# An mLSTM and sparse-attention layer step on one core: 66 of its 68 TensorE transposes are done by VectorE 32x32 turns and GpSimd copies, used three to five tiles later

## The chip, the cores and the metric

The kernel runs on one core of one Trainium2 chip. The metric is the device time of one execution in microseconds (us). PE is TensorE (PEld its weight loads), DVE is VectorE, ACT is ScalarE, POOL is GpSimd and SP is SyncE.

## The reference, cut to what matters

A step of a streaming encoder layer for 256 new frames (the prompt) and 32 frames of a running stream (the sample); every weight is shared by both.

```python
p = x @ w_in                                     # x: (288, 1024); about 12,000 columns
# branch B: 8 heads x 128, each query keeps its top keys by an indexer score
logits = where(kept, q @ k.T * 128**-0.5 + rel_bias, -inf)
o_b = softmax(logits) @ v
# branch A: mLSTM, 4 heads x 256, gates i and f
s = (q @ k.T) * wmat                             # decay weights, causal
h = (s @ v + (q * inter) @ C) / max(|s.sum + inter * q.n|, exp(-m))
C_new = decay * C + (w_s * k).T @ v              # n_new likewise
hn = (h - mean(h)) * rsqrt(var(h) + eps) * g     # per head and frame
branch_a = hn * sigmoid(o) * silu(z_a);  branch_b = o_b * silu(z_b)
y = layer_norm(alpha * x + (sigmoid(g_a) * (branch_a @ w_out_a)
                            + sigmoid(g_b) * (branch_b @ w_out_b)) @ w_o)
```

## The kernel before

The weights are cut into 117 tiles of 128 columns (or 128 rows), named by what they make and a number: `sm`, `qi`, then `qb`/`kb` by head, `vb`, `qa`/`ka`, `va`, `zb`, `oa`/`za`, `gb`/`wb`, `ga`/`wa`, `wo`. The main loop takes one tile at a time; a **slot** is one turn of it. Each f32 weight tile is split into a high part (`wh`, made by ACT in `split_hi`, L133) and a low part (`wl`, the rest, made by DVE in `split_lo`, L140), both of type fp32r, and each product is three matmuls: high by high, high by low of the other side, low by high (L901 to L903, 24 matmuls per tile). In slot t ACT makes `wh` of tile t+3 and DVE makes `wl` of tile t+2; there are two pairs of buffers (4 buffers of tag `wh`, 4 of `wl`). The slot before's product is then taken out of PSUM (`evac`), and the matmuls of tile t follow.

Halfway through a tile's 24 matmuls PE does side work: `side()` runs one step of every generator that is under way (`procs`), up to its next `yield`. A `yield` therefore means "in the next tile". Every engine takes its instructions in the order of this written program; what crosses engines is held by semaphores, and a buffer of a shared tag is taken again only when its last readers are done.

The side work that the change touches:

- `attn_sample`: softmax of the sample's logits (two groups of four heads, `lgs`), six PE transposes into PSUM (`aspt`, L517 and L519), ACT copies into `pst`, one tile later 48 small matmuls with the values (`os`, L531), two transposes back (`ost`, L540).
- `attn(h)`, eight heads, one started every two and a half tiles: logits (`al`), exponentials, normalised on DVE (L565), then one tile later three PE transposes (`apt`, L570); ACT takes the high part out of PSUM (`pth`, L573) and the plain part (`pt`, L574), DVE the low part (`ptl`, L575); one tile later the values' matmuls (`av`).
- `mlstm(h)`, four heads, one every four tiles: its normalised result `hn` (128 frames by 256) is transposed by four PE transposes (`ht`, L643) and multiplied on DVE out of PSUM (`ba`, L645).
- `k_weighted(h)`: four PE transposes (`kt`, L660) of the keys `kaT`, in the first four `wo` slots.
- `mlstm_sample`: two transposes of the sample's keys (`vks`, L742), the high and low parts of keys and values stacked in `stk` (the low parts by DVE, L756), the head norm with a power on POOL (L707), eight matmuls and eight DVE updates of the state (`stC`), two transposes at the end (`hts`, L785).

Of the kernel before, what the change touches and what calls it, by code (L numbers as in the profile page):

```python
# [10 lines left out]
F32 = mybir.dt.float32  # L11
# [9 lines left out]
TP = 256  # L21
# [65 lines left out]
def body(ctx, tc, a, o):  # L87
# [19 lines left out]
    def start(slot, gen):  # L107
        at(slot, procs.append, gen)

# [384 lines left out]
    def attn_sample():  # L494
# [5 lines left out]
        for g in two:  # L500
            lg = sb(f"lgs{g}", [128, 384], tag="lg", bufs=3)[:, :T]
            lgs.append(lg)
            st = sb(f"sts{g}", [128, 4], tag="st", bufs=3)
            dve.scalar_tensor_tensor(lg, q[g][:, :T], scale, bms[:, g], op0=OP.mult, op1=OP.add)
            dve.tensor_reduce(st[:, 0:1], lg, axis=AX.X, op=OP.max, negate=True)
            act.activation(lg, lg, AF.Exp, bias=st[:, 0:1], accum_out=st[:, 2:3])
            dve.reciprocal(st[:, 1:2], st[:, 2:3])
            dve.tensor_scalar(lg, lg, st[:, 1:2], None, op0=OP.mult)
        pts = [sb(f"pst{g}", [128, 384], tag="kw", bufs=2) for g in two]
        for g in two:  # L510
            dve.memset(pts[g][:, 256:384], 0.0)
        yield
# [7 lines left out]
        for g in two:  # L520
            act.copy(pts[g][:, 0:256], p[g][:, 0:256])
            for i in range(4):
                r = slice(32 * i, 32 * i + 32)
                act.copy(pts[g][r, 256 + 32 * i:288 + 32 * i], p[g][:TS, 256 + 32 * i:288 + 32 * i])
# [18 lines left out]
    def attn(h):  # L543
# [56 lines left out]
    def mlstm(h):  # L600
# [33 lines left out]
        yield  # L634
        while "state_done" not in store or cur[0] <= POS["za", 2 * h + 1] + 1:
            yield
        bah, bal = branch_a()
        ba = []
        for vb in range(2):
            p = bank(f"ht{h}{vb}")  # L640
            c = slice(128 * vb, 128 * vb + 128)
# [9 lines left out]

    def k_weighted(h):
# [4 lines left out]
        p = bank(f"kt{h}")  # L657
        for kd in range(2):
            for b in range(2):
                pe.transpose(p[:, 256 * b + 128 * kd:256 * b + 128 * kd + 128],  # L660
                             kaT[:, 2 * h + kd, 128 * b:128 * b + 128], ident)
        for b in range(2):
            k = slice(256 * b, 256 * b + 256)
            act.activation(kwh[:, b], p[:, k], AF.Identity, scale=gnat[:, b, 2, h:h + 1])
            dve.scalar_tensor_tensor(kwl[:, b], p[:, k], gnat[:, b, 2, h:h + 1], kwh[:, b].bitcast(F32),
                                     op0=OP.mult, op1=OP.subtract)
# [54 lines left out]
    def mlstm_sample():  # L721
# [3 lines left out]
        tail = sb("tail", [128, 2, 4, TS], tag="ba", bufs=2)  # L725
        for kd in range(2):
            pool.tensor_copy(tail[:, kd], kaT[:, kd:8:2, TP:T])
# [10 lines left out]
        p = bank("vks")  # L738
        v1 = sb("v1s", [128, 258], tag="v1s")
        dve.memset(v1[:, 256:258], 1.0)  # L740
        for kd in range(2):
            pe.transpose(p[:, 128 * kd:128 * kd + 128], tail[:, kd].rearrange("p h t -> p (h t)"), ident)  # L742
        act.copy(v1[:, 0:256], lazy["vas"])
        kw = sb("kws", [128, 258], tag="sw", bufs=2)
        dve.tensor_scalar(kw[:, 0:256], p[:, 0:256], gns[:, 2:3], None, op0=OP.mult)
# [4 lines left out]
        for i, (src, n) in enumerate(((kw, 256), (v1, 258))):  # L750
            act.copy(hi[i][:, :n], src[:, :n])
            for h in range(AH):
# [3 lines left out]
                dve.tensor_tensor(dst[lo:lo + 32], src[r, :n], hi[i][r, :n].bitcast(F32), OP.subtract)  # L756
# [26 lines left out]
        p = bank("hts")  # L783
        for vb in range(2):
            pe.transpose(p[:, 128 * vb:128 * vb + 128], hn[:, 0, 128 * vb:128 * vb + 128], ident)  # L785
        ba = sb("bas", [128, 2, 4, TS], tag="ba", bufs=2)
        for vb in range(2):
            dve.tensor_tensor(ba[:, vb], p[:, 128 * vb:128 * vb + 128].rearrange("p (h t) -> p h t", h=4),
                              GT[:, vb:8:2, TP:T], OP.mult)
# [278 lines left out]
    start(POS["zb", 2], mlstm_sample())  # L1068
    for h in range(AH):
# [129 lines left out]
```

## Time and profile before

| what | value |
|---|---|
| time, median of 3 runs | 425.77 us (425.51 to 426.06) |
| the profiled execution's own time | 425.51 us |
| its span in the trace | 423.8 us (1.7 us of the time lie outside) |
| PE busy | 417.5 us (99%) |
| DVE busy | 299.8 us (71%) |
| ACT busy | 227.1 us (54%) |
| POOL busy | 27.1 us (6%) |
| TensorE's granted clock over the span | 0.998 of full |

Busy time is the time in which an engine had an instruction under way; matmuls overlap each other, so the duration of one is longer than the step from one to the next. The step is read from the chain of work, the views that list times of start, and not from mean durations.

### The profile page before, as it was taken

Reading aid. Unit: us, or ns where it says so; the run is one execution under the profiler, and the core shown is the slowest. Engines: PE = TensorE matmul, PEld = TensorE weight load, DVE = VectorE, ACT = ScalarE, POOL = GpSimd, SP = SyncE. Lnnn points to the kernel's source line nnn. Section 1 sums busy time; section 2 is a strip of 40 time slices with the busy share of each in tenths; the row PEclk is TensorE's granted clock in tenths of the full one; section 3 lists DMA queues with packets and bytes.
Section 4 is the critical chain, followed back from the end, with each engine's and each line's share of the span. In section 5 each row is a group of like instructions: output and inputs, shape, how many; then the busy total and the mean of one; then the engine's idle time right before and its main releaser. Section 6 shows DMA issues by size and latency. Waiting matters only on the chain.

```text
span 423.8 us, 8154 instructions
## 1 busy us (share of the span) xinstructions
PE 417.5 (99%) x3180; PEld 394.3 (93%) x3180; DVE 299.8 (71%) x595; ACT 227.1 (54%) x443; POOL 27.1 (6%) x60
## 2 busy tenths in 40 slices
PE   8999999999999999999999999999999999999995
PEld 7999999778999998779999999999999999998864
DVE  5769999995856566675999987786444455665674
ACT  6775465326666565558796366545334344446402
POOL 0200011000400000000001101100000000000031
PEclk9999999999999999999999999999999999999999
DMA  8987979377954620437444454444645548433014
GB/s 310 378 296 215 316 252 330 123 199 265 388 164 149 215 87 0 174 126 298 150 149 150 151 181 167 151 149 150 198 150 171 177 150 281 154 125 124 28 38 150
DMA packets 31587, 78.70 MB, mean 186 GB/s; under 512 B 10412, under 2 KB 13724, under 8 KB 30748
## 3 DMA queue, kind: packets, MB, share of 16 engines
q1 hardware_dynamic: 30684, 76.86, 53.4%
q10 hardware_dynamic: 864, 1.32, 0.9%
q8 instruction: 25, 0.41, 0.4%
q14 instruction: 14, 0.11, 0.1%
HBM read 72.38 MB, written 7.68 MB: 189 GB/s over the span
## 4 chain that ended last, share of the span: by engine, by line
PE 97%; DVE 1%; POOLq 0%; ACT 0%; DVEq 0%; issue 0%
PE pj L902 22%; PE pj L901 22%; PE pj L903 22%; PE yn L949 5%; PE pj L968 3%; PE pj L919 2%; PE pj L918 2%; PE pj L917 2%; PE warm_p L151 1%; PE vap L917 1%; PE vbp L917 1%; PE vap L925 1%; PE vbp L925 1%; PE vbp L919 1%; PE vbp L918 1%; PE vap L919 1%
## 5 line engine op out<-in xcount | busy, mean ns | idle before, releaser
L133 ACT CAST wh<-wst 128x1024 fp32r<-128x1024 f32 x112 | 117.8, 1052 | 139.5 <-PE pj L902 68.2
L901 PE MATMUL pj<-xh,wh 128*128 128x288 f32 x576 | 171.1, 297 | 0.0
L902 PE MATMUL pj<-xl,wh 128*128 128x288 f32 x576 | 169.9, 295 | 0.0
L903 PE MATMUL pj<-xh,wl 128*128 128x288 f32 x576 | 169.7, 295 | 0.0
L140 DVE TENSOR_TENSOR wl<-wst,wh 128x1024 fp32r<-128x1024 f32 x112 | 136.2, 1218 | 30.6 <-ACT wh L133 30.2
L901 PEld LDWEIGHTS pj<-xh,wh 128*128 128x128 f32 x576 | 108.3, 188 | 0.5 <-issue 0.4
L902 PEld LDWEIGHTS pj<-xl,wh 128*128 128x128 f32 x576 | 108.3, 188 | 0.0
L903 PEld LDWEIGHTS pj<-xh,wl 128*128 128x128 f32 x576 | 108.2, 188 | 0.0
L902 PE MATMUL pj<-bbl,wh 128*128 128x288 f32 x64 | 18.9, 296 | 0.0
L903 PE MATMUL pj<-bah,wl 128*128 128x288 f32 x64 | 18.9, 296 | 0.0
L902 PE MATMUL pj<-bal,wh 128*128 128x288 f32 x64 | 18.9, 295 | 0.0
L901 PE MATMUL pj<-bbh,wh 128*128 128x288 f32 x64 | 18.9, 295 | 0.0
L901 PE MATMUL pj<-bah,wh 128*128 128x288 f32 x64 | 18.8, 294 | 0.0
L903 PE MATMUL pj<-bbh,wl 128*128 128x288 f32 x64 | 18.8, 294 | 0.0
L949 PE MATMUL yn<-wh,mxh 128*128 128x512 f32 x32 | 13.0, 406 | 0.0
L917 PE MATMUL pj<-wh,xh 128*128 128x512 f32 x32 | 12.9, 404 | 0.0
L949 PE MATMUL yn<-wl,mxh 128*128 128x512 f32 x32 | 12.6, 395 | 0.1
L919 PE MATMUL pj<-wh,xl 128*128 128x512 f32 x32 | 12.7, 395 | 0.0
L918 PE MATMUL pj<-wl,xh 128*128 128x512 f32 x32 | 12.6, 395 | 0.0
L949 PE MATMUL yn<-wh,mxl 128*128 128x512 f32 x32 | 12.6, 395 | 0.0
L901 PEld LDWEIGHTS pj<-bbh,wh 128*128 128x128 f32 x64 | 12.0, 188 | 0.0
L903 PEld LDWEIGHTS pj<-bah,wl 128*128 128x128 f32 x64 | 12.0, 188 | 0.0
(482 smaller groups left out, 674.5 us busy)
## 6 DMA issues: line engine op xcount, KB each, us to landing
wst<-in_w SPq DMA_DIRECT2D x112, 512.0 KB, 4.1
wst_k<-in_first SPq DMA_DIRECT2D x7, 464.0 KB, 4.3
rscr<-rrow SPq DMA_DIRECT2D x2, 768.0 KB
out_k<-kbT SPq DMA_DIRECT2D x1, 1152.0 KB
stC<-in_state_C SPq DMA_DIRECT2D x1, 1028.0 KB, 5.8
out_C_sample<-stC SPq DMA_DIRECT2D x1, 1028.0 KB
bm<-rscr SPq DMA_DIRECT2D x1, 1024.0 KB
ckT<-in_cache_k SPq DMA_DIRECT2D x1, 1024.0 KB
```

What stands on the lines that cost most here:

```text
L133: act.copy(split[t][0], stage[t])
L140: dve.tensor_tensor(wl, stage[t], wh.bitcast(F32), OP.subtract)
L151: pe.matmul(wp[:, :256], lhsT=warm[:, :128], rhs=warm, start=True, stop=True)
L901: pe.matmul(p[:, :T], lhsT=wh[:, c], rhs=h[:, k], start=(k == 0), stop=False)
L902: pe.matmul(p[:, :T], lhsT=wh[:, c], rhs=l[:, k], start=False, stop=False)
L903: pe.matmul(p[:, :T], lhsT=wl[:, c], rhs=h[:, k], start=False, stop=(k == KT - 1))
L917: pe.matmul(banks[i], lhsT=xh[:, k, r], rhs=wh[:, c], start=(k == 0), stop=False)
L918: pe.matmul(banks[i], lhsT=xh[:, k, r], rhs=wl[:, c], start=False, stop=False)
L919: pe.matmul(banks[i], lhsT=xl[:, k, r], rhs=wh[:, c], start=False, stop=(k == KT - 1))
L925: pe.matmul(banks[4][32 * i:32 * i + 32, 0:256].rearrange("p (g c) -> p g c", g=g), lhsT=xs0[:, kk], rhs=w[:, i], start=(kk == 0), stop=(k ...
L949: pe.matmul(p, lhsT=x[:, k, r], rhs=w[:, c], start=first and i == 0, stop=last and i == 2)
L968: pe.matmul(p[t][:, new], lhsT=w[:, 128 * t:128 * t + 128], rhs=x[:, k, new], start=(k == 0 and w is wh and x is xh), stop=(k == KT - 1 an ...
```

## The change

`carry` copies 32x32 blocks across groups of 32 partitions on POOL: four source groups by four target groups, 16 copies. A full transpose is now a DVE `transpose`, which turns each 32x32 block in its place, and then `carry`, which puts the blocks where they belong. All transposes of the list above but `ost` are done in this way, and each is used later by some `yield`s: the sample's probabilities 5 tiles after the softmax (3 before), a head's probabilities 3 tiles after the normalisation (1 before), `hn` 4 tiles after its turn. The sample's keys are turned at the start of `mlstm_sample` and used 4 tiles later (the whole of it now runs 3 tiles later from there on). The prompt's keys are turned in place by a new generator `k_natural`, 4 copies per tile over 16 tiles from `gb` 6, so that `k_weighted` has no PE work. The low parts in `stk` are made by POOL in place of DVE.

```diff
+    quads = tuple(slice(32 * i, 32 * i + 32) for i in range(4))
+    def carry(out, turned, rows):
+        for i in rows:
+            for k in range(4):
+                pool.tensor_copy(out(quads[k], quads[i]), turned(quads[i], quads[k]))
...
 attn_sample:
             dve.tensor_scalar(lg, lg, st[:, 1:2], None, op0=OP.mult)
+            dve.transpose(bms[:, g], lg)
...
-        yield
-        yield
-        p = [bank(f"aspt{g}") for g in two]
-        for g in two:
-            for b in two:
-                pe.transpose(p[g][:, 128 * b:128 * b + 128], lgs[g][:, 128 * b:128 * b + 128], ident)
-        for g in two:
-            pe.transpose(p[g][:TS, 256:384], lgs[g][:, 256:T], ident)
         for g in two:
-            act.copy(pts[g][:, 0:256], p[g][:, 0:256])
+            pt = pts[g][:, 0:256].rearrange("p (b k) -> p b k", b=2)
+            turned = bms[:, g, 0:256].rearrange("p (b k) -> p b k", b=2)
+            carry(lambda p, c: pt[p, :, c], lambda p, c: turned[p, :, c], range(4))
             for i in range(4):
-                r = slice(32 * i, 32 * i + 32)
-                act.copy(pts[g][r, 256 + 32 * i:288 + 32 * i], p[g][:TS, 256 + 32 * i:288 + 32 * i])
+                pool.tensor_copy(pts[g][quads[i], 256 + 32 * i:288 + 32 * i], bms[quads[i], g, 256:T])
+        yield
+        yield
+        yield
+        yield
         yield
         q = [bank(f"os{g}") for g in two]
...
 attn(h):
-        for i, s in enumerate(parts):
+        turned = bm[:, h].rearrange("p (c k) -> p c k", c=3)
+        for i, s, c in ((0, parts[0], slice(128, 384)), (1, parts[1], slice(0, 128))):
             dve.tensor_scalar(lg[:, s], lg[:, s], st[:, 2 + i:3 + i], None, op0=OP.mult)
+            dve.transpose(bm[:, h, c], lg[:, s])
+        ptf = sb(f"pt{h}", [128, 384], tag="kw", bufs=2)
+        pt3 = ptf.rearrange("p (c k) -> p c k", c=3)
+        carry(lambda p, c: pt3[p, :, c], lambda p, c: turned[p, :, c], range(4))
+        yield
+        yield
         yield
         vh, vl = two_parts(f"v{h}", vn[:, 0, 128 * h:128 * h + 128], "vph", "vpl")
-        p = bank(f"apt{h}")
-        for i, c in enumerate((256, 0, 128)):
-            pe.transpose(p[:, 128 * i:128 * i + 128], lg[:, c:c + 128], ident)
-        pt = sb(f"pt{h}", [128, 128], tag="sw", bufs=2)
+        pt = ptf[:, 256:384]
         ph, pl = (sb(f"pt{n}{h}", [128, 256], F32R, tag="hn", bufs=2) for n in "hl")
-        act.copy(ph, p[:, 0:256])
-        act.copy(pt, p[:, 256:384])
-        dve.tensor_tensor(pl, p[:, 0:256], ph.bitcast(F32), OP.subtract)
+        act.copy(ph, ptf[:, 0:256])
+        dve.tensor_tensor(pl, ptf[:, 0:256], ph.bitcast(F32), OP.subtract)
...
 mlstm(h):
+        for b in range(2):
+            dve.transpose(turned[:, b], hn[:, b])
...
+        carry(lambda p, c: hT[p, :, :, c], lambda p, c: turned[p, :, :, c], range(4))
+        for _ in range(4):
+            yield
...
-            for b in range(2):
-                pe.transpose(p[:, 128 * b:128 * b + 128], hn[:, b, c], ident)
-            dve.tensor_tensor(ba[vb], p[:, :TP], GT[:, 2 * h + vb, :TP], OP.mult)
+            dve.tensor_tensor(ba[vb], hn[:, vb], GT[:, 2 * h + vb, :TP], OP.mult)
...
+    def k_natural():
+        for h in range(AH):
+            k = kaT[:, 2 * h:2 * h + 2, 0:TP]
+            turned = sb(f"kn{h}", [128, 2, TP], tag="kw", bufs=2)
+            for i in range(2):
+                dve.transpose(turned[:, i], k[:, i])
...
+            for i in range(4):
+                carry(lambda p, c: kn[p, :, :, c], lambda p, c: turned[p, :, :, c], (i,))
+                yield
...
 mlstm_sample:
-                dve.tensor_tensor(dst[lo:lo + 32], src[r, :n], hi[i][r, :n].bitcast(F32), OP.subtract)
+                pool.tensor_tensor(dst[lo:lo + 32], src[r, :n], hi[i][r, :n].bitcast(F32), OP.subtract)
...
-        while cur[0] <= POS["za", 7] + 1:
+        while cur[0] <= POS["za", 7] + 6:
...
+    start(POS["gb", 6], k_natural())
```

**What stands in a row now, on PE.** This is PE in the tile that held the first head's transposes, before: `pj` is the tile's product, `apt` the transposed probabilities of head 0.

```order
L902 MATMUL pj_1774<-xl,wh_1606 128x288
L903 MATMUL pj_1774<-xh,wl_1607 128x288
L570 MATMUL apt_1791<-cst,lg_1659 128x128 x3
L901 MATMUL pj_1774<-xh,wh_1606 128x288
L902 MATMUL pj_1774<-xl,wh_1606 128x288
```

After the change the row `apt` is gone, with nothing in its place on PE; the same holds for `aspt`, `ht`, `kt`, `vks` and `hts`.

**On DVE, head 0's normalisation (`lg`), and the low part `ptl` that waits for the turned probabilities.** Before, from the normalisation of head 0 on:

```order
L565 TENSOR_SCALAR lg_1659<-lg_1659,st_1660 128x256
L565 TENSOR_SCALAR lg_1659<-lg_1659,st_1660 128x128
L555 SCALAR_TENSOR_TENSOR lg_1750<-al_1745,bm 128x384
L558 TENSOR_REDUCE st_1751<-lg_1750 128x1 x2
L140 TENSOR_TENSOR wl_1725<-wst_1417,wh_1724 128x1024
L477 TENSOR_TENSOR v0l<-vn,v0h 128x128
L575 TENSOR_TENSOR ptl_1797<-apt_1791,pth_1796 128x256
L140 TENSOR_TENSOR wl_1770<-wst_1455,wh_1769 128x1024
```

After the change, the same place up to `ptl` of head 0:

```order
L572 TENSOR_SCALAR lg_1653<-lg_1653,st_1654 128x256
L573 STREAM_TRANSPOSE bm<-lg_1653 128x256
L572 TENSOR_SCALAR lg_1653<-lg_1653,st_1654 128x128
L573 STREAM_TRANSPOSE bm<-lg_1653 128x128
...
L148 TENSOR_TENSOR wl_1715<-wst_1417,wh_1714 128x1024
L148 TENSOR_TENSOR wl_1809<-wst_1455,wh_1808 128x1024
...
L148 TENSOR_TENSOR wl_1847<-wst_1553,wh_1846 128x1024
L485 TENSOR_TENSOR v0l<-vn,v0h 128x128
L584 TENSOR_TENSOR ptl_1932<-pt_1767,pth_1931 128x256
L561 SCALAR_TENSOR_TENSOR lg_1940<-al_1935,bm 128x384
L564 TENSOR_REDUCE st_1941<-lg_1940 128x1 x2
L148 TENSOR_TENSOR wl_1909<-wst_1588,wh_1908 128x1024
```

Two turns were added behind the normalisation, and `ptl` moved behind three splits `wl` in place of one; the next split stands behind it as before.

**On POOL, from the causal masks of `wmat` to the first head norms (`dds`, `dd`).** Before:

```order
L361 AFFINE_SELECT wmat<-wmat 128x128 x8
L727 COPY tail<-kaT 128x128 x2
L594 MEMSET v1h 128x8x2
L595 MEMSET v1l 128x8x2
L707 TENSOR_TENSOR dds<-dds,mhalf 128x1
L707 TENSOR_TENSOR dd_3089<-dd_3089,mhalf 128x2
```

After the change, the same stretch:

```order
L369 AFFINE_SELECT wmat<-wmat 128x128 x8
L116 COPY pst_1497<-early 32x2x32 x16
L526 COPY pst_1497<-early 32x32 x4
L116 COPY pst_1498<-early 32x2x32 x16
L526 COPY pst_1498<-early 32x32 x4
L116 COPY pt_1767<-bm 32x3x32 x16
...
L116 COPY kn_s_2695<-kn_s_2696 32x2x32 x16
...
L777 TENSOR_TENSOR stk<-kws,hi_2941 32x256 x4
L777 TENSOR_TENSOR stk<-v1s,hi_2942 32x258 x4
L727 TENSOR_TENSOR dds<-dds,mhalf 128x1
L727 TENSOR_TENSOR dd_3213<-dd_3213,mhalf 128x2
L116 COPY hn_3214<-qaT 32x4x32 x16
```

POOL's queue, which held 12 instructions from the masks to the first power, now has 40 copies for the sample, 16 for each of eight heads (one row of them is shown), 16 for the sample's keys and 8 subtractions there, and 16 copies between one power and the next.

## Rows read from the trace of the kernel before

**Rows 1.** The page: the span, busy time of TensorE and of its weight loads with that of the others, and the chain that ended last, by engine.

```profile
span 423.8 us, 8154 instructions
PE 417.5 (99%) x3180; PEld 394.3 (93%) x3180; DVE 299.8 (71%) x595; ACT 227.1 (54%) x443; POOL 27.1 (6%) x60
PE 97%; DVE 1%; POOLq 0%; ACT 0%; DVEq 0%; issue 0%
```

**Rows 2.** The chain that ended last, in order of time (start us, us, what): the first and the last transposes of the attention heads (the other six `apt` rows read the same), one of the other kinds, and two pieces that mark a tile.

```profile
118.80 0.44 PE aspt L517 x4
122.63 1.45 PE os L531 x48
135.18 0.33 PE apt L570 x3
...
200.16 0.33 PE apt L570 x3
220.33 0.43 PE ns L762 x2
...
245.39 0.44 PE ht L643 x4
```

**Rows 3.** Groups of PE instructions by line (line, engine, op, out<-in, shapes, xcount | busy us, mean ns of one | idle before): four kinds of transposes. L519 and L785 are two more pairs like L742; L517 has the four of rows 2.

```profile
L570 PE MATMUL apt<-cst,lg 128*128 128x128 f32 x24 | 3.9, 272 | 0.0
...
L660 PE MATMUL kt<-cst,kaT 128*128 128x128 f32 x16 | 2.4, 272 | 0.0
L643 PE MATMUL ht<-cst,hn 128*128 128x128 f32 x16 | 2.4, 271 | 0.0
...
L742 PE MATMUL vks<-cst,tail 128*128 128x128 f32 x2 | 0.4, 272 | 0.0
```

**Rows 4.** The chain that ended last, at the only place in the middle of the program where it leaves PE (start us, us, what).

```profile
399.05 1.06 ACT wh L133
...
400.13 1.24 DVE wl L140
```

**Rows 5.** Who waited for whom (total us, times, longest us), the costliest row of ACT.

```profile
ACT wh L133 <- PE pj L902: 68.2, 45, 2.7
```

**Rows 6.** Groups of DVE instructions by line (as in rows 3): the split of a weight tile, the low parts of an attention head's probabilities, of its keys and of its values, and the sample's low parts.

```profile
L140 DVE TENSOR_TENSOR wl<-wst,wh 128x1024 fp32r<-128x1024 f32 x112 | 136.2, 1218 | 30.6 <-ACT wh L133 30.2
...
L575 DVE TENSOR_TENSOR ptl<-apt,pth 128x256 fp32r<-128x256 f32 x8 | 3.4, 423 | 5.1 <-ACT pt L574 3.0 <-PE al L483 2.0
...
L756 DVE TENSOR_TENSOR stk<-kws,hi 32x256 fp32r<-32x256 f32 x4 | 1.7, 418 | 0.1
...
L477 DVE TENSOR_TENSOR k1l<-kbT,k1h 128x256 fp32r<-128x256 f32 x1 | 0.4, 426 | 0.0
...
L477 DVE TENSOR_TENSOR v1l<-vn,v1h 128x128 fp32r<-128x128 f32 x1 | 0.3, 292 | 0.6 <-ACT v1h L476 0.6
```

**Rows 7.** Groups of POOL instructions by line: a two-input addition, and copies of 32 and of 128 elements per partition.

```profile
L876 POOL COPY mxs<-sg 128x32 f32<-128x32 f32 x8 | 1.7, 211 | 97.2 <-DVE sg L875 97.2
...
L419 POOL TENSOR_TENSOR accs<-accs,srel 64x288 f32<-64x288 f32 x1 | 0.9, 883 | 28.8 <-ACT accs L418 28.8
...
L727 POOL COPY tail<-kaT 128x128 f32<-128x128 f32 x2 | 0.6, 294 | 47.2 <-ACT kaT L835 47.2
```

**Rows 8.** POOL in order of time (start us, us, instruction and count): the same masks of `wmat` at two places.

```profile
102.93 0.54 POOL L361 TENSOR_SCALAR_AFFINE_SELECT wmat<-wmat 128x128 f32<-128x128 f32 x2 [36.58 <-ACT wmat L359]
106.68 2.04 POOL L361 TENSOR_SCALAR_AFFINE_SELECT wmat<-wmat 128x128 f32<-128x128 f32 x2 [3.21 <-ACT wmat L359]
```

**Rows 9.** DVE in order of time around those masks (in brackets the idle time before it and what ended it).

```profile
105.51 1.23 DVE L140 TENSOR_TENSOR wl<-wst,wh 128x1024 fp32r<-128x1024 f32 x1 [4.00 <-ACT wh L133]
106.65 1.92 DVE L450 TENSOR_TENSOR bm<-bm,mk 128x768 f32<-128x768 f32 x2
...
109.83 0.95 DVE L450 TENSOR_TENSOR bm<-bm,mk 128x768 f32<-128x768 f32 x1
```

**Rows 10.** POOL in order of time near the end: four copies of one element per partition from the last group of 32 partitions to each of the four.

```profile
411.75 0.90 POOL L1041 COPY nr<-mv 32x1 f32<-32x1 f32 x4
```

**Rows 11.** DVE in order of time from the first normalised probabilities of the sample on: the pieces that are longest.

```profile
113.71 0.37 DVE L508 TENSOR_SCALAR lgs<-lgs,sts 128x288 f32<-128x288 f32 x1
...
116.40 2.29 DVE L140 TENSOR_TENSOR wl<-wst,wh 128x1024 fp32r<-128x1024 f32 x2
...
122.48 1.22 DVE L140 TENSOR_TENSOR wl<-wst,wh 128x1024 fp32r<-128x1024 f32 x1
...
126.02 1.22 DVE L140 TENSOR_TENSOR wl<-wst,wh 128x1024 fp32r<-128x1024 f32 x1
```

**Rows 12.** PE in order of time: the last matmul of a tile's first half and the side work that follows it, two tiles after the tile of `os`.

```profile
131.13 0.29 PE L903 MATMUL pj<-xh,wl 128*128 128x288 f32 x1
131.26 0.38 PE L551 MATMUL al<-kbT,qbT 128*128 128x128 f32 x2
```

**Rows 13.** DVE in order of time from the second `zb` tile to the first `za` tile: the last idle time before, the normalisation of head 7, one split, and the first idle time over 0.5 us after.

```profile
197.54 0.46 DVE L848 TENSOR_TENSOR sg<-pj,sg 128x288 f32<-128x288 f32 x1 [2.14 <-ACT sg L847]
...
198.60 0.55 DVE L565 TENSOR_SCALAR lg<-lg,st 128x256 f32<-128x256 f32 x2
...
213.19 1.22 DVE L140 TENSOR_TENSOR wl<-wst,wh 128x1024 fp32r<-128x1024 f32 x1
...
229.18 0.52 DVE L858 SCALAR_TENSOR_TENSOR sg<-pj,ang,sg 128x288 f32<-128x288 f32 x1 [0.78 <-ACT sg L857]
```

More of the change, by code (lines that the diff above doesn't have):

```diff
@@ L511, in attn_sample @@
             dve.memset(pts[g][:, 256:384], 0.0)
+        for g in two:
+            pt = pts[g][:, 0:256].rearrange("p (b k) -> p b k", b=2)
[3 more added lines that the diff above has]
+                pool.tensor_copy(pts[g][quads[i], 256 + 32 * i:288 + 32 * i], bms[quads[i], g, 256:T])
         yield
         yield
[L514 to L524 removed]
+        yield
+        yield
         yield
@@ L650, in mlstm @@
             dve.tensor_tensor(bal[:, j, :TP], ba[vb], bah[:, j, :TP].bitcast(F32), OP.subtract)
+    def k_natural():
[4 more added lines that the diff above has]
+                dve.transpose(turned[:, i], k[:, i])
+            turned = turned.rearrange("p d (b k) -> p b d k", b=2)
+            kn = k.rearrange("p b (d k) -> p b d k", d=2)
+            for i in range(4):
+                carry(lambda p, c: kn[p, :, :, c], lambda p, c: turned[p, :, :, c], (i,))
+                yield
     def k_weighted(h):
@@ L656, in k_weighted @@
         kwh, kwl = lazy["kwh"][:, h], lazy["kwl"][:, h]
[L657 to L661, printed above, removed]
         for b in range(2):
-            k = slice(256 * b, 256 * b + 256)
-            act.activation(kwh[:, b], p[:, k], AF.Identity, scale=gnat[:, b, 2, h:h + 1])
-            dve.scalar_tensor_tensor(kwl[:, b], p[:, k], gnat[:, b, 2, h:h + 1], kwh[:, b].bitcast(F32),
+            k = kaT[:, 2 * h + b, 0:TP]
+            act.activation(kwh[:, b], k, AF.Identity, scale=gnat[:, b, 2, h:h + 1])
+            dve.scalar_tensor_tensor(kwl[:, b], k, gnat[:, b, 2, h:h + 1], kwh[:, b].bitcast(F32),
                                      op0=OP.mult, op1=OP.subtract)
@@ L724, in mlstm_sample @@
         s = lazy["ss"]
-        tail = sb("tail", [128, 2, 4, TS], tag="ba", bufs=2)
+        kn, turned = (sb(f"kn_s{i}", [128, 2, 128], tag="ba", bufs=2) for i in range(2))
         for kd in range(2):
-            pool.tensor_copy(tail[:, kd], kaT[:, kd:8:2, TP:T])
+            dve.transpose(turned[:, kd].rearrange("p (h t) -> p h t", h=4), kaT[:, kd:8:2, TP:T])
+        carry(lambda p, c: kn[p, :, c], lambda p, c: turned[p, :, c], range(4))
         sw = sb("sws", [128, 128], tag="sw", bufs=2)
@@ L737, in mlstm_sample @@
         yield
-        p = bank("vks")
         v1 = sb("v1s", [128, 258], tag="v1s")
         dve.memset(v1[:, 256:258], 1.0)
-        for kd in range(2):
-            pe.transpose(p[:, 128 * kd:128 * kd + 128], tail[:, kd].rearrange("p h t -> p (h t)"), ident)
         act.copy(v1[:, 0:256], lazy["vas"])
+        yield
+        yield
+        yield
         kw = sb("kws", [128, 258], tag="sw", bufs=2)
-        dve.tensor_scalar(kw[:, 0:256], p[:, 0:256], gns[:, 2:3], None, op0=OP.mult)
+        dve.tensor_scalar(kw[:, 0:256], kn.rearrange("p d k -> p (d k)"), gns[:, 2:3], None, op0=OP.mult)
         yield
@@ L778, in mlstm_sample @@
         at(cur[0] + 2, lambda: sp.dma_start(o["C_sample"], stC))
-        while cur[0] <= POS["za", 7] + 1:
+        while cur[0] <= POS["za", 7] + 6:
+            yield
+        turned = qs.rearrange("p (d h) t -> p d (h t)", d=2)
+        hT = hn[:, 0].rearrange("p (d k) -> p d k", d=2)
+        for vb in range(2):
+            dve.transpose(turned[:, vb], hT[:, vb])
+        carry(lambda p, c: hT[p, :, c], lambda p, c: turned[p, :, c], range(4))
+        for _ in range(4):
             yield
@@ L782, in mlstm_sample @@
         bah, bal = branch_a()
-        p = bank("hts")
-        for vb in range(2):
-            pe.transpose(p[:, 128 * vb:128 * vb + 128], hn[:, 0, 128 * vb:128 * vb + 128], ident)
         ba = sb("bas", [128, 2, 4, TS], tag="ba", bufs=2)
         for vb in range(2):
-            dve.tensor_tensor(ba[:, vb], p[:, 128 * vb:128 * vb + 128].rearrange("p (h t) -> p h t", h=4),
+            dve.tensor_tensor(ba[:, vb], hT[:, vb].rearrange("p (h t) -> p h t", h=4),
                               GT[:, vb:8:2, TP:T], OP.mult)
```

5 lines of the change are left out of this document (3 added, 2 removed).

## The prediction

> **What bounds the kernel now.** The page comes first: TensorE is busy 99% of a span of 423.8 us, and the chain that ended last is TensorE's for 97% [rows 1]. The next question is whether anything stands close behind it. The waits say no: ScalarE's costliest wait is for TensorE to give back a weight buffer (68.2 us in 45 waits), so the split of the weights runs as far ahead as its buffers let it [rows 5]. VectorE waits 30.6 us for ScalarE's half of that split [rows 6]. Every piece of side work on TensorE therefore adds its own time to the end, and taking it away gives that time back, as long as the split and the other engines keep up.
>
> How much they may lag is the margin of a split. `ns` starts at 220.33, in the middle of tile `oa` 0 [rows 2]. Twelve matmuls lie ahead of it in that tile, one every 0.13 us [rows 12], so the tile began near 218.8. VectorE makes one `wl` per slot; counted back from there, this tile's is the one that started at 213.19 and took 1.22 us [rows 13]. The margin is 4.3 us, and this is at the end of a stretch, 197.5 to 228, in which VectorE never waits for over 0.5 us [rows 13].
>
> **Removed from TensorE.** 24 + 16 + 16 + 4 and three pairs are 66 transposes [rows 2, 3]. Their mean duration of 272 ns overlaps with their neighbours'; the chain has 0.33 us for three and 0.44 for four, 0.11 us each [rows 2]. So 66 x 0.11 = 7.26 us go, and nothing is put on TensorE. The profiled execution of 425.51 us would take 418.25; the median is 0.26 above it, hence 418.5 from 425.77 before any new wait. The place where the chain leaves TensorE late in the program (ACT `wh`, DVE `wl`, 2.3 us) begins with TensorE giving back a buffer [rows 4], so it only moves forward with the rest, and so does the ending behind it.
>
> **ScalarE** loses copies out of PSUM and is not near the bound: nothing.
>
> **Added to VectorE: 38 turns.** No row shows one. The nearest are 0.42 us for 256 columns and 0.29 for 128 (one tensor against another) [rows 6]; half of it and twice it are my bounds. I take the rows themselves, with no reason to lean to either bound. That is 0.71 us per attention head. Removed are eight subtractions of 0.418 us, 3.35 us [rows 6].
>
> **Added to GpSimd: 328 copies and 8 subtractions.** Copies of 32 and 128 elements take 0.211 and 0.294 us [rows 7], so 64 elements 0.24 and 96 elements 0.27. Two masks start 0.25 us apart where each lasts some 0.29 (0.54 for both) [rows 8]; four copies between groups of partitions took 0.90, some 0.22 each at one element [rows 10]. A head's 16 copies thus take 3.5 us (0.22 each) to 4.9 us (0.31) undisturbed. They are not undisturbed: the same pair of masks took 0.54 us while VectorE was idle (4.00 us of idle time end at 105.51) and 2.04 us beside VectorE's `bm` additions [rows 8, 9]. Instructions of VectorE that read two tensors in SBUF and GpSimd's instructions wait for each other, and one of GpSimd's passes between two of VectorE's. VectorE loses little by it: 1.92 us for the two additions against 2 x 0.95 [rows 9]; I take up to 0.1 us per copy, with 0.01 and the whole copy of 0.27 as bounds.
>
> Does GpSimd keep up? Heads follow each other every (200.16 - 135.18) / 7 = 9.28 us [rows 2], 8.95 without the transposes. In that time VectorE holds the access for 2.5 splits (3.05 us), the normalisation (0.55, counted to be safe), and four low parts of query, key, values and probabilities (0.29 + 0.43 + 0.29 + 0.42) [rows 6, 13]: 5.0 us in 8.5 instructions. The 3.9 us left hold 12 to 17 copies, and 8 more pass between instructions: 20 to 25 for 16. `ptl`, in whose queue the next `wl` stands behind it, reads them three tiles after the turn, 10.7 us by the same rate. They come in time.
>
> The sample's 40 copies have the shortest time. They can start at 114.1 (113.71 + 0.37) [rows 11], and `os` stands two tiles later than before, at 131.26 [rows 12] less the 0.66 us of six removed transposes, 130.6: 16.5 us. VectorE holds the access for 0.37 + 2.29 + 1.22 + 1.22 us [rows 11] and 1.4 us of query and key low parts of two heads, 6.5 in all; the copies need 7.4 (0.18 each) to 11 us (0.275). The sum is 13.9 to 17.5: TensorE waits 0 to 1.0 us.
>
> In the dense stretch up to 228 VectorE gains the turns of head 7 (0.71) and of the sample's keys (0.58) and the delayed low parts of head 6 (0.71), up to 3.2 us from 32 copies at 0.1, and what eight two-input subtractions on GpSimd hold (0.883 us each alone [rows 7]; 0 to 0.5 each for VectorE). It loses 3.35. The net is 2 to 6 us later, 2 likelier, against a margin of 4.3: TensorE waits 0 to 1.7 us. `hn` has four tiles and the prompt's keys five for copies of 4 to 5.3 us, so nothing waits there.
>
> Sum: 418.5 plus 0.3 for short waits, **418.8 us**.
>
> The Trainium skill, SBUF — State Buffer, section "Who interferes with whom", says that whichever of the two engines starts first keeps the shared access for its whole instruction and the other blocks fully. By that rule, with no part of two instructions overlapping, the outcome is rival (a) below, 418.5 + 2.8 = 421.3 us from the heads alone. The masks that waited agree with it in kind; the additions beside them, which lost almost nothing, do not agree in size.
>
> **The rivals.** (a) *The access is too dear.* If copies and VectorE's instructions exclude each other in full, a head needs 5.0 + 16 x 0.27 = 9.3 us of 8.95, 0.35 us late each, 2.8 us for eight; `os` waits its 1.0, and the dense stretch its 1.7. With one to all of these the time is 419.8 to 424.0. For it: the masks at 1.02 us each. Against: what VectorE lost there.
>
> (b) *No change*: all of (a), and turns at twice my price on top, which in the dense stretch and the heads behind it (whose eight turns cost 3.4 us more) leave VectorE the bound: 425 to 426.5. Against: over the whole span VectorE is idle for 29% [rows 1].
>
> (c) *Slower*, by GpSimd alone, at the attention heads. Lateness adds up from head to head once a copy takes over 8.95 / 16 = 0.56 us, and it costs more than the gain plus the margin (7.3 + 4.3 = 11.6 us over eight heads, 1.45 each) from (8.95 + 1.45) / 16 = 0.65 us on. At the 1.02 us of the masks it would be 16.3 us per head, 59 us late, some 473 us. For it: that row is the only one beside a busy VectorE. Against: there VectorE held the access without a pause, here for 5.0 of 8.95 us, and when VectorE itself waits for `ptl` it holds nothing.
>
> **How the numbers follow.** My forecast (418.0 to 419.8) 0.64, (a) 0.23, (b) 0.04, (c) 0.09. Faster means by over 0.2%, 0.85 us, about the least that a measurement of this kernel can tell: 0.64 + 0.23 = 0.87; the same 0.04; slower 0.09. The range begins at 418.0, half a microsecond under the sum without any wait, and reaches into (a) to 422.5, which leaves out the rest of (a), (b) and (c), some 0.17.
>
> **What the changed profile would show.** Right: TensorE with 66 matmuls fewer and still 99% busy, no wait on TensorE at `os` over 1 us, and no ScalarE wait for `pt` of several us. A head's 16 copies within 8 us; a pair of turns near 0.7 us. Wrong: waits of PE `pj` for DVE `wl` between 200 and 290 (then it is (a) by the dense stretch); waits of ACT `pth` for POOL that grow from head to head ((c)); a TensorE wait at `os` ((a) by the sample).

## The result, and the profile after

The changed kernel takes **423.50 us** (median of 4 runs, 423.35 to 423.53) against 425.74 for the kernel before beside it: ratio 0.9946, 95% interval 0.9929 to 0.9963. It is faster, by 2.2 us where 7 were forecast, and lies outside the range given (418.0 to 422.5).

The page of the changed kernel, profiled at 423.53 us: span, engines, the chain that ended last by engine, and three groups (busy us, mean ns | idle time before and what ended it).

```profile
span 421.8 us, 8381 instructions
PE 411.8 (98%) x3114; PEld 387.5 (92%) x3114; DVE 313.8 (74%) x625; ACT 223.2 (53%) x425; POOL 176.7 (42%) x394
PE 91%; DVE 3%; ACT 2%; DMA 1%; issue 1%; POOLq 0%; DVEq 0%; ACTq 0%
...
L926 PE MATMUL pj<-xh,wh 128*128 128x288 f32 x576 | 171.1, 297 | 2.9 <-DVE sg L873 2.6
...
L148 DVE TENSOR_TENSOR wl<-wst,wh 128x1024 fp32r<-128x1024 f32 x112 | 137.7, 1234 | 23.5 <-ACT wh L141 23.1
...
L116 POOL COPY pt<-bm 32x96 f32<-32x96 f32 x128 | 50.1, 391 | 24.3 <-DVE bm L573 19.1
```

Beside [rows 1, 6]: the 66 matmuls are gone, POOL went from 6% to 42%, the split `wl` is 16 ns slower, and TensorE's share of the chain fell from 97% to 91%. What is new is an idle time in front of L926, the first matmul of a product: it waits for `sg` of DVE, L873. In the list of waits (total us, times, longest), the waits of TensorE and of its weight loads for a product's bank; the kernel before has none of them:

```profile
PE pj L926 <- DVE sg L873: 2.6, 2, 1.5
PE pj L926 <- ACT kaT L860: 0.2, 1, 0.2
PEld pj L926 <- DVE sg L873: 3.6, 4, 1.7
PEld pj L926 <- ACT kaT L860: 0.4, 1, 0.4
```

`sg` L873 is the multiplication with which `evac` takes a `zb` product out of PSUM. The products share two PSUM banks (`out_bank`, tag `proj`, `bufs=2`), so tile t+1 may begin only when tile t-1 has been evacuated; and that evacuation stands in slot t on DVE behind the side work of slot t-1 and behind `wl` of tile t+2.

To count what was lost, each step of TensorE (start of one matmul to start of the next) is set against the median step of the same kind in the kernel before. The last transpose of most groups has a step of only 0.03 us, but the first matmul behind it has a longer one (a product's 0.22 for 0.13), so a group is counted from the matmul ahead of it to the third behind it: the 66 transposes make 7.23 us. The last matmul ends at 416.16 us; before it was 418.69. The change touches nothing in the first 113 us, which took 0.24 us longer in this execution. From the same product matmul on (113.08 us in the kernel before) to the start of the last matmul it is 302.56 us for 305.32. So 2.76 us arrived and 4.47 were lost: 1.74 us at the tile behind 203.2, 1.45 at 221.4, 0.44 at 117.2, 0.32 at 195.7, 0.24 at 199.2, all for a bank (at 117.2 for ScalarE's evacuation `kaT`), and 0.27 in the steps of `os`.

### The profile page after: what moved, and what is told of

Same layout as the page of the kernel before. It is cut to its first block, busy times and chain, and to the rows that moved or that the text cites. A ratio compares the mean times of both kernels' runs of the same rounds, so it can differ in the third digit from the quotient of the medians.

```text
span 421.8 us, 8381 instructions
## 1 busy us (share of the span) xinstructions
PE 411.8 (98%) x3114; PEld 387.5 (92%) x3114; DVE 313.8 (74%) x625; ACT 223.2 (53%) x425; POOL 176.7 (42%) x394
## 4 chain that ended last, share of the span: by engine, by line
PE 91%; DVE 3%; ACT 2%; DMA 1%; issue 1%; POOLq 0%; DVEq 0%; ACTq 0%
PE pj L926 21%; PE pj L927 21%; PE pj L928 21%; PE yn L974 5%; PE pj L993 3%; PE pj L944 2%; PE pj L943 2%; PE pj L942 2%; ACT wh L141 1%; PE vap L942 1%; PE vbp L942 1%; DMA wst_k<-in_first 1%; PE vbp L944 1%; PE vbp L950 1%; PE vap L950 1%
## 5 line engine op out<-in xcount | busy, mean ns | idle before, releaser
L926 PE MATMUL pj<-xh,wh 128*128 128x288 f32 x576 | 171.1, 297 | 2.9 <-DVE sg L873 2.6
L148 DVE TENSOR_TENSOR wl<-wst,wh 128x1024 fp32r<-128x1024 f32 x112 | 137.7, 1234 | 23.5 <-ACT wh L141 23.1
L926 PEld LDWEIGHTS pj<-xh,wh 128*128 128x128 f32 x576 | 108.6, 188 | 4.6 <-DVE sg L873 3.6
L116 POOL COPY pt<-bm 32x96 f32<-32x96 f32 x128 | 50.1, 391 | 24.3 <-DVE bm L573 19.1
L116 POOL COPY kaT<-kn 32x128 f32<-32x128 f32 x64 | 32.7, 511 | 21.9 <-DVE kn L670 19.3
L116 POOL COPY hn<-qaT 32x128 f32<-32x128 f32 x48 | 24.0, 500 | 18.8 <-DVE qaT L646 16.9
L369 POOL TENSOR_SCALAR_AFFINE_SELECT wmat<-wmat 128x128 f32<-128x128 f32 x8 | 4.9, 640 | 41.9 <-ACT wmat L367 41.9
L926 PE MATMUL pj<-bah,wh 128*128 128x288 f32 x64 | 18.8, 294 | 0.0
L926 PE MATMUL pj<-bbh,wh 128*128 128x288 f32 x64 | 18.8, 294 | 0.0
L1024 POOL TENSOR_TENSOR nr<-mv,mhalf 128x1 f32<-128x1 f32 (+1 forms) x3 | 4.0, 1349 | 24.3 <-DVE mv L1023 24.3
L116 POOL COPY pst<-early 32x64 f32<-32x64 f32 x32 | 12.4, 387 | 2.5 <-DVE early L517 1.1
L427 POOL TENSOR_TENSOR accs<-accs,srel 64x288 f32<-64x288 f32 x1 | 0.9, 887 | 28.6 <-ACT accs L426 28.6
```

What stands on the lines that cost most here:

```text
L116: pool.tensor_copy(out(quads[k], quads[i]), turned(quads[i], quads[k]))
L148: dve.tensor_tensor(wl, stage[t], wh.bitcast(F32), OP.subtract)
L926: pe.matmul(p[:, :T], lhsT=wh[:, c], rhs=h[:, k], start=(k == 0), stop=False)
```

## The experiments

All twelve in one table. "Last matmul" (its end) and "lost" are from the profiled execution: lost is what the removed transposes make (7.23 us; 4.58 in e10, none in e2 and e6) less what the stretch from 113 us to the last matmul became shorter. The first 113 us, ahead of all that the change touches, differ by up to 0.8 us from one execution to the next; the times and the column "last matmul" hold that too.

| kernel | time, us | ratio to before, 95% | last matmul, us | lost from 113 us on, us |
|---|---|---|---|---|
| changed | 423.50 | 0.9929 to 0.9963 | 416.16 | 4.47 |
| e1: third bank | 421.28 | 0.9878 to 0.9905 | 413.63 | 2.26 |
| e2: third bank, kernel before | 425.62 | 0.9984 to 1.0002 | 418.40 | -0.10 |
| e3: sample's mLSTM later | 421.31 | 0.9876 to 0.9906 | 414.16 | 2.30 |
| e4: low parts on DVE | 422.78 | 0.9912 to 0.9937 | 415.46 | 3.73 |
| e5: no copies | 421.97 | 0.9899 to 0.9926 | 414.66 | 3.42 |
| e6: before, only the later use | 426.94 | 1.0017 to 1.0037 | 420.21 | 0.98 |
| e7: e1 + e3 | 421.24 | 0.9881 to 0.9908 | 413.41 | 2.21 |
| e8: e1 + e3 + e4 | 421.09 | 0.9877 to 0.9908 | 413.80 | 2.23 |
| e9: e1, av and os a tile later | 418.83 | 0.9829 to 0.9856 | 411.30 | -0.13 |
| e10: heads' transposes on PE | 423.66 | 0.9942 to 0.9967 | 416.66 | 2.46 |
| e11: e9 + e3 | 418.76 | 0.9822 to 0.9849 | 411.26 | -0.13 |
| e12: e9, no copies | 419.12 | 0.9824 to 0.9851 | 411.90 | -0.15 |

### Is it the bank? e1 and e2

```diff
-        return ps.tile([128, 512], F32, name=name, tag="side", bufs=6)
+        return ps.tile([128, 512], F32, name=name, tag="side", bufs=5)
...
-        return ps.tile([128, 512], F32, name=f"pj{t}", tag="proj", bufs=2)
+        return ps.tile([128, 512], F32, name=f"pj{t}", tag="proj", bufs=3)
```

> The changed kernel with three PSUM banks for the projections' products instead of two, taken from the six of the other tiles (five are left). Theory 1 (the gain was lost where a product's first matmul waits until the product two tiles earlier has been evacuated from the same bank, 4.2 us in all over the starts of five tiles): the waits at the tiles starting at 195.7, 199.2, 203.2 and 221.4 us vanish or shrink to a tenth, and the time is about 419.3 to 420.5 us, near the forecast. Theory 2 (VectorE's added turns, the lock waits and stretched operations are the loss themselves, so that the low parts of the split tiles come late): the wait moves from the bank to the low part of the split sample or weight tile at the same place, and the time stays 423 to 424 us. If five banks are too few for the other tiles, TensorE waits for those instead, which would show as a wait at their first matmul.

> The kernel before with the same exchange of one bank. Control for the run with three banks of the changed kernel: in the kernel before no tile but a few starts with a wait for its bank, so both theories expect no change, 425.3 to 426.0 us; a gain here of over 1 us would mean that the third bank gives something that has nothing to do with the change.

e1 took 421.28 us and e2 425.62. Every wait for a bank is gone from e1, and the same edit gives the kernel before nothing: theory 1, as to the cause, though the time is not in its band. e1 gained 2.2 us and not 4.2, because waits came up that the bank's had covered. In e1's list of waits, TensorE's for `ptl`, and from its tile `pst` the copies behind which `os` (its `vs` part up to 130.8) ran out (duration min/median/max, first and last start):

```profile
PE av L490 <- DVE ptl L584: 1.0, 2, 0.7
PEld av L490 <- DVE ptl L584: 1.4, 2, 1.0
...
L116 POOL COPY pst<-early x31: 226/232/1263, 114.9 to 129.3; 32x64 f32<-32x64 f32 x31
L526 POOL COPY pst<-early x8: 199/202/207, 122.1 to 130.4; 32x32 f32<-32x32 f32 x8
```

By steps these are 0.39 us at head 6 and 0.90 at head 7 (each with 0.1 more beside the next matmul), and 0.85 spread over the `os` matmuls, the last of which follow the copies at 0.13 us each where four of them took 0.11 before. In the changed kernel, where TensorE comes to `os` later, it is 0.27, and in e5 below, without copies, nothing.

### Is it where the sample's mLSTM stands? e3 and e7

```diff
-    start(POS["zb", 2], mlstm_sample())
+    start(POS["zb", 3], mlstm_sample())
```

> The changed kernel with the sample's mLSTM started one projection tile later (at zb 3 instead of zb 2), and nothing else. Theory 1a (the two large waits, 1.74 us at 203.2 and 1.45 us at 221.4, come from the sample's work meeting the last attention head's turns and, later, the first prompt head's scaled queries and keys): both shrink, about 420.5 to 421.5 us. Theory 2 (the turns and copies cost what they cost wherever they stand): 423 to 424 us. If one tile later meets other work, a wait of 1 us or more appears at another tile's start.

> The changed kernel with the third bank and with the sample started one tile later. The third bank alone leaves waits for the low part of heads 6 and 7 (0.39 and 0.90 us beside the first matmuls of their products) and 0.7 us at the sample's scores. If the first two are from the sample's start beside the last heads' turns, as the run with the later start says, they go and the time is 420.0 to 420.4 us. If the two edits cure the same loss only, the time is that of the better one, 421.3 us.

e3 took 421.31 us, as theory 1a had it; the two large waits give way to one at another tile:

```profile
PE pj L926 <- DVE sg L873: 0.7, 1, 0.7
```

By its step it is 0.90 us (0.11 more beside the second matmul), behind 206.56, where the sample's start now stands. e7 refuted the reason I gave for the waits of heads 6 and 7: with the sample later they are the same, 0.40 and 0.86 us. The two edits cure the same loss. `ptl` is late because it is made in the tile ahead of `av`, behind the evacuation, whatever the sample does.

### What makes the evacuation late? e5, e10, e6

e5 leaves GpSimd's copies out:

```diff
     def carry(out, turned, rows):
-        for i in rows:
-            for k in range(4):
-                pool.tensor_copy(out(quads[k], quads[i]), turned(quads[i], quads[k]))
+        return
...
```

Where a later step needs the copied tile, the turn writes that tile itself.

> The changed kernel without GpSimd's 306 block copies (272 would be the same argument): VectorE's turns stay, and where a later step needs the copied tile the turn writes that tile itself. It leaves out the exchange of the 32 x 32 blocks, so its values are not the reference's; everything else, the later places of the users and GpSimd's low parts too, is as in the changed kernel. Theory A (the two large waits come from what VectorE and ScalarE do in these tiles, the moved work and the turns themselves): the waits at 203.2 and 221.4 us stay within 0.5 us of 1.74 and 1.45, and the time is 422.7 to 423.5 us. Theory B (GpSimd's copies hold VectorE back, by waits for the shared port and by stretched operations): the wait at 203.2 us shrinks under 0.6 us and the time is 421.0 to 422.0 us. Under either, the sample's pst, 15.7 us of copies in the changed kernel, no longer holds the sample's scores back.

(The count of 306 in it is wrong, and so is the remark behind it: the groups of the trace add up to 328.) e10 gives the heads' transposes back to TensorE:

```diff
 attn(h):
-            dve.transpose(bm[:, h, c], lg[:, s])
...
-        carry(lambda p, c: pt3[p, :, c], lambda p, c: turned[p, :, c], range(4))
-        yield
-        yield
...
+        p = bank(f"apt{h}")
+        for i, c in enumerate((256, 0, 128)):
+            pe.transpose(p[:, 128 * i:128 * i + 128], lg[:, c:c + 128], ident)
```

> The changed kernel with two banks, but the eight attention heads as before: their 24 transposes on TensorE, their users two tiles earlier. 24 transposes of about 0.11 us are given back (2.6 us); the rest of the change stands. If head 7's turns and the users of head 6, moved two tiles later, make the evacuation late that the tile at 203.2 us waits for, that wait falls from 1.74 to under 0.5 us and the time is 423.4 to 424.5 us, though TensorE has 2.6 us more to do. If the sample's start alone makes it late, the wait stays and the time is 425 to 426 us.

e6 is the kernel before with the later users alone, of which this is two places:

```diff
...
 attn(h):
+        yield
+        yield
         yield
         vh, vl = two_parts(f"v{h}", vn[:, 0, 128 * h:128 * h + 128], "vph", "vpl")
...
 mlstm_sample:
+        yield
+        yield
+        yield
+        p = bank("vks")
...
```

> The kernel before, all its transposes still on TensorE, with nothing of the change but the later use: two tiles more ahead of the sample's transposes and of each attention head's, four ahead of a prompt head's, three ahead of the sample's keys, nine ahead of the sample's last transposes. No turns, no copies, low parts on VectorE. Theory A (moved work that meets other work is enough to make evacuations late): waits for the bank at the tiles of the sample's start or of the first prompt head, 1 to 3 us in all, and 426.5 to 428.5 us. Theory B (it takes the turns, or the 0.44 us per head that TensorE no longer spends): 425.6 to 426.2 us, no wait for a bank over 0.3 us.

Times 421.97, 423.66 and 426.94 us. The waits of TensorE for `sg` in the three, in this order (L869, L870 and L857 are L873's line there):

```profile
PE pj L922 <- DVE sg L869: 2.2, 2, 1.2
```

```profile
PE pj L923 <- DVE sg L870: 1.2, 1, 1.2
```

```profile
PE pj L910 <- DVE sg L857: 0.4, 1, 0.4
PEld pj L910 <- DVE sg L857: 0.9, 2, 0.6
```

The last line is e6's wait of the weight loads: there are two. Without copies the wait at 203 falls from 1.74 to 1.31 us (1.20 beside the first matmul, 0.11 beside the second) and that at 221 stays at 1.46: theory A by the waits, though the time is in the band of theory B, since the wait at 117 (0.44) and the lost steps of `os` (0.27) went too and 0.5 us are of the first 113 us. Without the heads' turns and copies (e10) the wait at 203 falls to 0.32 us (0.22 beside the first matmul, a step at 205.7), those at 195.7 and 199.2 are gone, and 117 and 221 remain. The 24 transposes cost TensorE 2.65 us and end 2.0 us of waits; the end of the program is 0.3 us shorter, and the time is that of the changed kernel within 0.2 us.

The later use alone (e6) costs the kernel before 1.3 us, 0.98 of it from 113 us on. That is two waits for a bank, 0.32 us (a step at 197.9) and 0.63 (at 222.5), at the tiles that wait at 195.7 and 221.4 in the changed kernel. Theory B (no wait over 0.3) is out, and A holds, its 1 us just missed by 0.05. So these two tiles lose this much without a turn or a copy, and with all transposes still on TensorE; at the tile of 203.2, where the changed kernel loses most, e6 loses nothing.

### GpSimd's subtractions: e4 and e8

```diff
-                pool.tensor_tensor(dst[lo:lo + 32], src[r, :n], hi[i][r, :n].bitcast(F32), OP.subtract)
+                dve.tensor_tensor(dst[lo:lo + 32], src[r, :n], hi[i][r, :n].bitcast(F32), OP.subtract)
```

> The changed kernel with the sixteen low parts of the sample's keys and values subtracted on VectorE again, as in the kernel before, and all else as changed. If GpSimd's subtractions, 871 to 954 ns each, hold back VectorE beside them (three operations there are 1.37 us longer than their like elsewhere), the wait at 221.4 us shrinks from 1.45 to under 0.5 us and the time is 422.3 to 423.0 us. If VectorE's own load there is what makes the evacuation late, giving it sixteen more subtractions of about 0.35 us makes the wait longer, and the time 424 to 426 us. If neither, 423.5 us.

> The same with the sample's sixteen low parts on VectorE again. With a third bank there is no wait left at the place that GpSimd's subtractions stretched, so this should give nothing beside the run without it: within 0.3 us of it. If VectorE's lateness there is still carried on into a later wait, 0.3 to 0.7 us faster.

(There are eight of them, not sixteen.) e4 took 422.78 us, as the first case had it: the wait at 221.4 falls from 1.45 to 0.61 us, a little above the 0.5 expected. What is left is the 0.63 us that e6 has at the same tile. In order of time, first the changed kernel's POOL subtractions and the DVE operations beside them, then e4's DVE:

```profile
217.35 3.66 POOL L777 TENSOR_TENSOR stk<-kws,hi 32x256 fp32r<-32x256 f32 x4 [3.62 <-ACT hi L772]
```

```profile
217.49 0.99 DVE L828 TENSOR_TENSOR bbl<-sg,bbh 128x288 fp32r<-128x288 f32 x1
219.43 0.98 DVE L485 TENSOR_TENSOR qa0l<-qaT,qa0h 128x512 fp32r<-128x512 f32 x1 [0.96 <-ACT qa0h L484]
220.33 0.96 DVE L485 TENSOR_TENSOR ka0l<-kaT,ka0h 128x256 fp32r<-128x256 f32 x1
```

```profile
217.59 0.45 DVE L828 TENSOR_TENSOR bbl<-sg,bbh 128x288 fp32r<-128x288 f32 x1
218.06 0.85 DVE L777 TENSOR_TENSOR stk<-kws,hi 32x256 fp32r<-32x256 f32 x2
219.54 0.69 DVE L485 TENSOR_TENSOR qa0l<-qaT,qa0h 128x512 fp32r<-128x512 f32 x1 [0.63 <-ACT qa0h L484]
220.15 0.42 DVE L485 TENSOR_TENSOR ka0l<-kaT,ka0h 128x256 fp32r<-128x256 f32 x1
```

The three operations take 0.99 + 0.98 + 0.96 us beside GpSimd and 0.45 + 0.69 + 0.42 without it, 1.37 us more, while the two subtractions that DVE does there itself cost it 0.85 in a gap that it had. The third bank takes the value out of it: e8 is within 0.15 us of e7.

### The waits underneath: e9, e11, e12

e9 is e1 with two `yield`s more:

```diff
...
 attn_sample:
         yield
+        yield
         q = [bank(f"os{g}") for g in two]
...
 attn(h):
         dve.tensor_tensor(pl, ptf[:, 0:256], ph.bitcast(F32), OP.subtract)
+        yield
         yield
         c = slice(128 * h, 128 * h + 128)
...
```

> The run with the third bank, and two users moved one projection tile later: each attention head's products with its values (av), and the sample's scores with its values (os). With three banks the profile still shows waits of 0.39 and 0.86 us for the low part of heads 6 and 7 (ptl, ready in the same tile as av) and 0.7 us at os behind the last of 40 copies of pst. If these are what is left of the loss, they vanish, TensorE's work ends 1.9 us earlier, and the time is 419.2 to 419.8 us, in the range that was forecast (418.0 to 422.5). If there are no waits but the time stays at 421.3 us, something else sets the end.

> The run with the third bank and the users of the heads and of the sample's scores one tile later, with the sample's mLSTM one tile later too. If nothing waits any more in either, the same time as without the later start, within 0.3 us, 419.2 to 419.8 us.

> The fastest of the kernels so far (third bank; av and os one tile later; 418.83 us) without GpSimd's 328 block copies (an earlier expectation gave 306; the rows of the trace of the changed kernel add up to 328). It leaves out the exchange of the 32 x 32 blocks, so its values are not the reference's. If the copies' 1.03 us between 113 and 240 us that the run without them gained over the changed kernel were lost only where a product waited for its bank, nothing is left to gain here: 418.4 to 419.0 us. If GpSimd's copies slow something that still sets the end (VectorE's operations beside them, the weights' transfers), 417.3 to 418.2 us.

e9 took **418.83 us**, 1.6% below the kernel before; that is the time that was forecast for the change without these edits. Its page, and the one wait of TensorE's matmuls that its list has left, at the program's start, where the kernel before has it too:

```profile
span 417.1 us, 8386 instructions
PE 410.1 (98%) x3114; PEld 387.1 (93%) x3114; DVE 314.7 (75%) x625; ACT 223.7 (54%) x425; POOL 178.5 (43%) x394
```

```profile
PE warm_p L159 <- DVE warm L154: 1.1, 1, 1.1
```

All of it arrives: from 113 us on TensorE's work is 7.36 us shorter. That was a little better than expected (419.2 to 419.8). e11 (418.76) adds nothing. e12 (419.12, above the 418.4 to 419.0 expected for no difference) gains nothing without the copies: its first 113 us took 0.6 us longer than e9's, and from there to the last matmul it is 297.94 us, with the copies (e9) 297.96. Once nobody waits for them they cost no time. The turns and copies were affordable all along; where their users and the banks stood was not. No run has the later users with two banks, so how much of e9 they would give by themselves is not shown.

## Why the prediction was wrong, point by point

**The work removed: right.** The 66 transposes make 7.23 us where 7.26 were taken (0.11 us each), and e9 shows that they can all be had.

**The price of turns and copies: right.** From the tiles `bm` and `pt` of the changed kernel (min/median/max):

```profile
L116 POOL COPY pt<-bm x128: 257/262/1354, 130.9 to 204.9; 32x96 f32<-32x96 f32 x128
L573 DVE STREAM_TRANSPOSE bm<-lg x16: 311/380/446, 129.6 to 197.6; 128x256 f32<-128x256 f32 x8, 128x128 f32<-128x128 f32 x8
```

A pair is 0.45 + 0.31 = 0.76 us (0.71 taken), a copy 0.26 undisturbed (0.27). In a head 16 copies are busy 50.1 / 8 = 6.3 us of the 8.95 there are. No head falls behind: rival (c) is out, and so is that part of (a). The split waits for no copy, and no ScalarE wait for one shows. At `os` TensorE loses 0.27 us (0 to 1.0 taken), 0.85 when it comes there 0.75 us earlier (e1). TensorE is 98% busy, not 99.

**The margin: wrong, and this is the step that failed.** The prediction took 4.3 us as the slack of the dense stretch, from `wl` of the tile, and set 2 us of lateness against it. That reading is right: counted tile by tile, `wl` lies 4.2 to 5.6 us ahead there, and in the changed kernel it is done 4.3 us before TensorE comes to the tile that waits at 203.2. But `wl` is not what stands closest behind TensorE. The kernel before shows it, one row of DVE and one of PE that I had not set side by side: the evacuation that frees the bank, and the first matmul of the tile that takes it.

```profile
204.83 0.46 DVE L848 TENSOR_TENSOR sg<-pj,sg 128x288 f32<-128x288 f32 x1
```

```profile
205.89 0.29 PE L901 MATMUL pj<-xh,wh 128*128 128x288 f32 x1
```

It ends at 205.29: the margin was 0.60 us. At the tile that now waits at 221.4 it was 0.37 (evacuated at 223.03, taken at 223.40). The same place in the changed kernel, DVE from the last idle time on, with what is new, and the weight load that waits:

```profile
195.51 0.46 DVE L873 TENSOR_TENSOR sg<-pj,sg 128x288 f32<-128x288 f32 x1 [4.66 <-ACT sg L872]
...
196.96 0.45 DVE L573 STREAM_TRANSPOSE bm<-lg 128x256 f32<-128x256 f32 x1
...
197.61 0.31 DVE L573 STREAM_TRANSPOSE bm<-lg 128x128 f32<-128x128 f32 x1
...
200.51 0.52 DVE L584 TENSOR_TENSOR ptl<-pt,pth 128x256 fp32r<-128x256 f32 x1
200.95 0.49 DVE L747 STREAM_TRANSPOSE kn_s<-kaT 128x128 f32<-128x128 f32 x2
...
202.42 0.78 DVE L756 TENSOR_TENSOR qs<-qaT,qscale 128x64 f32<-128x64 f32 x4
203.13 1.28 DVE L148 TENSOR_TENSOR wl<-wst,wh 128x1024 fp32r<-128x1024 f32 x1
204.44 0.46 DVE L873 TENSOR_TENSOR sg<-pj,sg 128x288 f32<-128x288 f32 x1
```

```profile
204.95 0.19 PEld L926 LDWEIGHTS pj<-xh,wh 128*128 128x128 f32 x1 [1.71 <-DVE sg L873]
```

Counted from the evacuation two tiles before (197.54 in [rows 13], 195.51 here), DVE's run to the freed bank took 7.75 us and now takes 9.39 (to 204.90). In e5, without copies, it takes 9.02: of the 1.64 us more, 1.27 are the turns (0.45 + 0.31 + 0.49 by their rows) and 0.37 are operations that copies stretch (`ptl` 0.52 for 0.41, the four `qs` 0.78 for 0.63, `bbl`, `v6l` and `wl` by 0.06 each). This lateness is near the 2 us that the prediction held likelier; what it was set against is not. The weight load follows 0.05 us behind the evacuation, at 9.44. TensorE without its transposes wanted the bank 7.81 us after the same point (203.19 and one step of 0.13), before 8.35. So the wait is 9.44 - 7.81 = 1.63 us beside the first matmul, as measured (1.64). In e5 it is 1.20; e10 takes the heads' part away, gives TensorE's transposes back, and 0.22 us are left. The removed work shortens TensorE's side of the race as well: of the 0.60 us of margin, 0.54 went with the transposes themselves.

**"VectorE gains 2 to 6 us in the dense stretch, TensorE waits 0 to 1.7": wrong in the place and in the sum.** It named `wl` between 200 and 290 as what would show it; what showed was `sg`, 1.74 + 0.32 + 0.24 us up to 203 and 1.45 at 221, 3.75 in all. At 221 the moved work met other work: the later use alone loses 0.63 us at this tile (e6). That it comes from `stk` and its high parts, which hold ScalarE ahead of `qa0h`, is read from DVE's idle time there (0.63 us in e6, 0.45 before) and not tested. GpSimd's subtractions stretch DVE by 1.37 us: that is 0.84 of the 1.45 (e4). The sum credited VectorE with 3.35 us for eight subtractions that it no longer does; the two that stand there cost it nothing, since they fill a gap (e4), and the credit bought nothing at this bank. The low end of "2 to 6" also counts all 32 copies at 0.1 us; by the prediction's own bound of 0.01 it is 1 us earlier instead of 2 later.

**"Come in time" for the heads: true for the copies, not for `ptl`.** The subtraction stands in the tile ahead of its user as before, but `ptl` now comes behind a later evacuation. The wait was covered by the bank's until e1 took that away.

**The rivals.** The time lies in the band of (a), but not by its mechanism: exclusion in full, adding up over the heads, is not there. The copies are 1.05 us of the 4.47 (e5) and nothing in e12. The Trainium skill, SBUF — State Buffer, section "Who interferes with whom", says that an instruction of VectorE with both inputs in SBUF contends with one of GpSimd that reads SBUF. e4's rows agree with it for GpSimd's long subtractions. For the copies the price falls on GpSimd: 16 of the heads' 128 copies take over 1 us, and each of them overlaps a split `wl` of 1.2 to 1.3 us, while the rows above show a loss of 0.06 to 0.11 us for an instruction of VectorE, under a copy's 0.26.

**The rest of the miss.** 418.8 to 423.5 is 4.7 us: 4.47 lost where 0.3 were taken, 0.24 in the first 113 us of the profiled execution, and about 0.5 at the ending, which was taken to move forward unchanged: from the last matmul to the end of the span 5.1 us before and 5.6 after. These make 4.9; the profiled execution of before lies 0.2 to 0.3 under its median, which takes that back. That e9 meets the forecast to 0.1 us is in part luck: its last matmul comes 7.39 us earlier, and 0.7 of it goes again at the ending (5.8).

## What to carry to other kernels

Where TensorE is the bound, ask for every tile which release ends last before its first matmul, and take the smallest margin of them: buffers of the next operand, the PSUM bank, the operand made in the tile before. Here the weights ran 4 us ahead and the bank 0.6, and the side work put on VectorE was paid for at the bank. A third bank and one tile more for two users made the change worth 6.8 us instead of 2.2 (e9), and the bank alone gave the kernel before nothing (e2): slack is bought where a trace shows its margin, not in general. The Trainium skill, Perfetto Trace Analysis, section "Matmuls", asks for matmul groups that rotate through several banks so that an evacuation lies under the next group; in this kernel two were enough before the change and not after it.

## What the runs showed of the hardware that I had not expected

A turn costs VectorE about what a two-input operation of that size costs there, 0.45 us for 256 columns and 0.31 for 128 (0.42 and 0.29 in [rows 6]). One copy of GpSimd beside a busy VectorE has a wide spread (257 to 1354 ns at a median of 262), so that the mean (391) is 1.5 times the median, and the few that meet a split `wl` set when a set of copies is complete: 5.9 to 7.9 us for the 16 of a head.

The end of the span: `out_y` took longer to land, in the views of DMA issues of the kernel before and of the changed one (last number: us from issue to landing).

```profile
out_y<-z__4809 SPq DMA_DIRECT2D x4, 256.0 KB, 3.5
```

```profile
out_y<-z__5091 SPq DMA_DIRECT2D x4, 256.0 KB, 4.0
```

From the last matmul to the end of the span it is 5.1 to 5.3 us in the three kernels with all transposes on TensorE and 5.3 to 5.8 in those with turns. The chain of work puts the difference behind the last instruction of DVE (4.6 us to the end of the span before, 5.1 after). Nothing behind the first four `wo` tiles was changed, and no run tells why; this stays open.
